# Compressed keys behind every block of the window keys: one logit product for two attention branches

## The chip, the cores and the metric

The program runs on one core of one Trainium2 chip. The core's engines run beside each other, each with its own queue of instructions: PE (TensorE) multiplies matrices, ACT (ScalarE) applies functions, DVE (VectorE) and POOL (GpSimd) work element by element, and SP (SyncE) issues transfers between the chip's memory and the on-chip memory. The metric is the time of one execution in microseconds; less is better.

## The reference

One transformer block on a sequence of 1024 tokens with a model width of 1024: a norm, one large input projection, two mixers beside each other (an mLSTM and a sparse attention), a gated merge of both, and a feed-forward network. The change lies in the sparse attention. It has 8 query heads of width 64 in 2 key groups, and for each query it sums three branches:

```python
def block(i):
    ...
    lc = (jnp.einsum('bgrqd,bgcd->bgrqc', qb, kc_).astype(jnp.float32)
          + table[:, :, rel_bucket(t[:, None] - cmp_end[None, :])])
    p_c = masked_softmax(lc, cmp_end[None, :] <= t[:, None])
    o_c = jnp.einsum('bgrqc,bgcd->bgrqd', p_c, vc_.astype(jnp.float32))
    ...
    ls = jnp.einsum('bgrqd,bgqnd->bgrqn', qb, k_g).astype(jnp.float32) + bias_s
    p_s = masked_softmax(ls, mask_s[:, :, None])
    o_s = jnp.einsum('bgrqn,bgqnd->bgrqd', p_s, v_g.astype(jnp.float32))
    ...
    lw = jnp.einsum('bgrqd,bgkd->bgrqk', qb, k_wb).astype(jnp.float32) + table[:, :, rel_bucket(dist)]
    p_w = masked_softmax(lw, mask_w)
    o_w = jnp.einsum('bgrqk,bgkd->bgrqd', p_w, v_wb.astype(jnp.float32))
    gb = lax.dynamic_slice_in_dim(gates, qs, Q, axis=3)
    return gb[..., 0:1] * o_c + gb[..., 1:2] * o_s + gb[..., 2:3] * o_w
```

The compressed branch (c) attends to 63 compressed keys, each made from 32 tokens by a small network. The selected branch (s) attends to the top 16 blocks of 64 tokens; with 1024 tokens these are all blocks, so it is plain causal attention. The window branch (w) attends to the last 512 tokens. `masked_softmax` divides by `max(sum, 1e-30)`, and `gates` is a sigmoid of a projection.

## The kernel before

**Stages.** The program runs in stages, one after the other with some overlap: the norm and the transposed input; the projections and the mLSTM; B2, which makes the queries of the attention and the compressed keys and values; C, the attention; the rest of the merge, the output projection and the feed-forward network. Each product in high precision is made from parts: a float32 operand is split into a rounded high part and the low rest (names in `H`/`hi` and `L`/`lo`), and a product is two or three matmuls.

**B2** (from some 315 to 380 us). `b2_dense` makes the four query tiles `nq`, each in two halves of 512 tokens. A half comes out of PSUM by ACT as `st` (printed as `snq`), DVE rounds it to `hnq` and takes the rest `lnq`, and SP stores both to memory (`d_qh`, `d_ql`). Beside it, `compress` adds positions to the raw keys (`fl`, sixteen DVE steps), multiplies with `w_cmp1` (`ph`) and writes the compressed keys as `KHC` and `KLC` (64 columns for each key group) and the values as `VHC`. Weights stream in through `raw` tiles, loaded by SP in pieces of 512 bytes, and are split into `whi` (ACT) and `wlo` (DVE or, in C, POOL). After the first query tile, `load_pair(0)` asks POOL's queue for the queries of the first pair of heads (`QA`) and the keys of the first group (`KH`, `KL`, in rows of 4 KB; j = 1 are the window's, j = 0 the selected branch's), and SP's for the tables of position biases (`FB`, `FW`).

**C** (from some 382 to 707 us) has 32 units: 4 pairs of heads p, and for each the 8 blocks i of 128 queries in the order 0, 7, 1, 6, 2, 5, 3, 4. A unit u has five jobs: the window product for both heads, the compressed product for both heads together, the selected product for both heads. A job runs on PE (`s_job`: L974 and L975 with the high and low keys, L960 and L961 with the compressed ones, into a PSUM tile `S`), on DVE (L987: add the bias, clip, row minimum into `nx`) and on ACT (L991: exponential and row sum `sm`). `scale` makes the factor `rs` = gate / max(sum, 1e-30) in three DVE steps (L1003 to L1005), once for the window and compressed branch and once for the selected one, and multiplies it in. `t_job` transposes the weights on PE (`T`, L1043), copies them as `TH` (ACT, L1048) and `TL` (DVE, L1052), and multiplies with the values into `obank` (L1063, L1065); ACT takes the result out as `os` (L1071), and SP stores it.

**The order in C** is set when the program is built, by a list scheduler: each operation has an engine, an assumed duration and what it depends on, and the operation that can start first is emitted next. Where PE would wait, `place_dense` puts in three matmuls of the merge projection (`d`, nine tiles, 420 matmuls in C) as filler; a tile's half leaves as `mg` (L922). When the last product of a pair has been read by DVE, `load_pair` asks for the next pair's data, and for new keys after the second pair.

## Time and profile before

| | |
|---|---|
| median of 3 runs | 1622.4 us (1619.43 to 1623.4) |
| profiled execution, its own time | 1624.57 us |
| span of its trace | 1622.8 us |
| granted PE clock, mean | 0.991 |
| busy share of the span | PE 97%, DVE 66%, ACT 46%, POOL 13% |
| chain that ended last | PE 82%, DVE 4%, DMA 3%, ACT 1% |

The span is the time from the first to the last instruction of one profiled execution on the slowest core. A busy time adds up the durations of an engine's instructions, and PE's matmuls overlap, so the distance from one start to the next says more about their price than their duration. A wait is the idle time of an engine before an instruction, put down to what ended it.

### The profile page before, as it was taken

What the parts mean: (1) busy time and instruction counts of PE and PEld (TensorE: products, weight loads), DVE (VectorE), ACT (ScalarE), POOL (GpSimd) and SP (SyncE); (2) the same over time, 40 slices, a digit from 0 to 9 for tenths busy, and PEclk for the clock granted to TensorE, in tenths of its full rate; (3) what the DMA queues carried; (4) which work ended last, traced back from release to release, by engine and by line L of the source; (5) the groups of instructions that cost most, each with busy time, mean ns of one, the idle gap of its engine ahead of it and who ended that gap; (6) DMA issues with size and microseconds to landing.
All of it is one profiled execution on the core that took longest, in us unless ns stands there. A gap on an engine that the chain in (4) does not pass through costs nothing.

```text
span 1622.8 us, 22113 instructions
## 1 busy us (share of the span) xinstructions
PE 1572.2 (97%) x7938; PEld 1327.5 (82%) x7938; DVE 1066.4 (66%) x2276; ACT 746.6 (46%) x1561; POOL 204.5 (13%) x225
## 2 busy tenths in 40 slices
PE   6999999989999999999999998999999999999997
PEld 6876888878989888988887887888888888888876
DVE  6456553245888687952355378666676666978996
ACT  5225455325878687853334344333333333454443
POOL 4002333310102110012000014000000000000130
PEclk9999999999999999999999999999999999999999
DMA  8003532782233422154447222222332223741202
GB/s 251 7 22 97 150 116 96 240 242 70 67 101 82 125 66 82 40 173 148 143 139 255 74 85 85 78 87 89 118 103 78 79 78 104 285 166 42 98 7 104
DMA packets 143773, 181.43 MB, mean 112 GB/s; under 512 B 10414, under 2 KB 100944, under 8 KB 143664
## 3 DMA queue, kind: packets, MB, share of 16 engines
q1 hardware_dynamic: 137440, 157.31, 31.5%
q0 software_dynamic: 5888, 22.06, 4.8%
q8 instruction: 62, 1.02, 0.3%
q10 hardware_dynamic: 336, 0.66, 0.1%
q14 instruction: 47, 0.39, 0.1%
HBM read 137.95 MB, written 49.90 MB: 116 GB/s over the span
## 4 chain that ended last, share of the span: by engine, by line
PE 82%; DVE 4%; DMA 3%; ACT 1%; issue 1%; SPq 0%; POOL 0%; DVEq 0%; ACTq 0%
PE PS L271 14%; PE PS L272 14%; PE PS L270 14%; PE d L270 6%; PE d L272 6%; PE d L271 6%; PE T L1043 4%; PE obank L1063 2%; PE obank L1065 2%; PE br L270 1%; PE br L271 1%; PE br L272 1%; DMA raw<-in_w_in 1%; PE pn L696 1%; DMA q<-d_yn 0%
## 5 line engine op out<-in xcount | busy, mean ns | idle before, releaser
L270 PE MATMUL d<-UTH,whi 128*128 128x512 f32 x576 | 235.1, 408 | 3.4 <-ACT snq L846 2.4
L272 PE MATMUL d<-UTH,wlo 128*128 128x512 f32 x576 | 227.1, 394 | 1.1 <-POOL wlo L249 1.1
L271 PE MATMUL d<-UTL,whi 128*128 128x512 f32 x576 | 226.1, 393 | 0.0
L1421 DVE TENSOR_TENSOR sl<-PS,sl 128x512 f32<-128x512 f32 x182 | 124.0, 688 | 100.2 <-PE PS L272 98.4
L272 PEld LDWEIGHTS d<-UTH,wlo 128*128 128x128 f32 x576 | 108.9, 189 | 26.1 <-POOL wlo L249 1.9
L270 PEld LDWEIGHTS d<-UTH,whi 128*128 128x128 f32 x576 | 109.2, 190 | 21.9 <-ACT snq L846 3.0
L249 POOL TENSOR_TENSOR wlo<-raw,whi 128x1024 fp32r<-128x1024 f32 x31 | 76.2, 2458 | 402.5 <-ACT whi L247 308.2
L271 PEld LDWEIGHTS d<-UTL,whi 128*128 128x128 f32 x576 | 109.6, 190 | 17.6
L1052 DVE TENSOR_TENSOR TL<-T,TH 128x512 fp32r<-128x512 f32 (+1 forms) x184 | 103.7, 583 | 20.9 <-ACT TH L1048 19.5
L1048 ACT ACTIVATE TH<-T 128x512 fp32r<-128x512 f32 (+1 forms) x184 | 90.8, 511 | 34.4 <-PE T L1043 31.6
L1421 DVE TENSOR_TENSOR sl<-sl,sl 128x512 f32<-128x512 f32 (+1 forms) x113 | 77.3, 691 | 18.3 <-ACT sl L1424 12.9
L1424 ACT ACTIVATE sl<-sl 128x512 f32<-128x512 f32 (+1 forms) x85 | 53.5, 631 | 69.8 <-PE PS L271 47.6
L1063 PE MATMUL obank<-TH,VHL 128*128 128x256 f32 x264 | 76.4, 312 | 0.0
L1424 ACT ACTIVATE wh<-sl 128x512 fp32r<-128x512 f32 x61 | 38.5, 631 | 81.9 <-PE PS L271 71.6
L1421 POOL TENSOR_TENSOR acc<-acc 128x512 f32<-128x512 f32 x6 | 9.2, 1548 | 503.5 <-DVE acc L1421 503.4
L1065 PE MATMUL obank<-TL,VHL 128*128 128x256 f32 x264 | 68.5, 282 | 0.0
L270 PE MATMUL PS<-q 128*128 128x512 f32 x172 | 66.9, 389 | 0.0
L271 PE MATMUL PS<-q 128*128 128x512 f32 x172 | 66.9, 389 | 0.0
L272 PE MATMUL PS<-q 128*128 128x512 f32 x172 | 66.9, 389 | 0.0
L1383 DVE TENSOR_TENSOR q<-br,q 128x512 f32<-128x512 f32 x32 | 21.9, 688 | 67.3 <-ACT q L1376 47.0
L1424 ACT ACTIVATE q<-sl 128x512 fp32r<-128x512 f32 x74 | 43.4, 624 | 46.5 <-PE PS L271 29.1
L1421 DVE TENSOR_TENSOR q<-sl,q 128x512 fp32r<-128x512 f32 x72 | 50.3, 736 | 2.9 <-ACT q L1424 2.9
(1418 smaller groups left out, 4302.0 us busy)
## 6 DMA issues: line engine op xcount, KB each, us to landing
raw<-in_w_in SPq DMA_DIRECT2D x40, 512.0 KB, 4.7
ra<-in_w_gate SPq DMA_DIRECT2D x22, 512.0 KB, 5.3
d_gu<-sl SPq DMA_DIRECT2D x44, 256.0 KB, 2.1
q<-d_mg SPq DMA_DIRECT2D x32, 256.0 KB, 3.2
d_rep<-d_row POOLq DMA_DIRECT2D x8, 960.0 KB, 10.0
sl<-d_gu SPq DMA_DIRECT2D x15, 512.0 KB, 5.3
sl<-in_w_down SPq DMA_DIRECT2D x15, 512.0 KB, 5.2
ra<-in_w_up SPq DMA_DIRECT2D x11, 512.0 KB, 3.8
```

Of the source, the lines that this page charges most:

```text
L249: eng.tensor_tensor(lo, v, cast32(hi), ALU.subtract)
L270: nc.tensor.matmul(ps, ah, bh, start=first, stop=False)
L271: nc.tensor.matmul(ps, ah, bl, start=False, stop=False)
L272: nc.tensor.matmul(ps, al, bh, start=False, stop=last)
L1043: nc.tensor.transpose(pt[:, z, P * r:P * r + P], e, ident)
L1048: nc.scalar.activation(hl[0][:, 0:m], pt[:, 0:m], AF.Copy)
L1052: nc.vector.tensor_tensor(hl[1][:, 0:m], pt[:, 0:m], cast32(hl[0])[:, 0:m], ALU.subtract)
L1063: nc.tensor.matmul(po, vv, th[:, z, :], start=(st[1] == 0), stop=False)
L1065: nc.tensor.matmul(po, vv, tl[:, z, :], start=False, stop=(st[1] == st[2]))
L1383: nc.vector.tensor_tensor(sg[b], ps, sg[b], ALU.mult)
L1421: return pl.step(alts, lambda e: ENG[e].tensor_tensor(out_(), x(), y(), alu), reads, writes, **kw)
L1424: return pl.step((("ACT", cost),), lambda e: nc.scalar.activation(out_(), x(), fn), reads, writes, **kw)
```

## The change

The tile of the window keys gets 192 instead of 128 columns for each block of 128 keys. The new function `behind` copies the group's 64 compressed keys behind each of the eight blocks on POOL: for the first group after B2, for the second in `load_pair`. The last block of a window product then is 192 columns wide and gives the logits of the window and of the compressed branch for that head at once; the compressed product as a job of its own goes. The earlier blocks of the window stand in a product of their own. The loads of the window keys, split in blocks now, move in pieces of 512 bytes. The gates are inverted once after the sigmoid, so that a factor is 1 / (max(sum, 1e-30) x inverted gate): one fused DVE step and a reciprocal in place of three. Five tiles lose a buffer: `lnq` and `snq` in B2, `mg` and `os` in C. The scheduler's assumed durations are changed with it, and with them its order.

```diff
@@ -30,6 +30,7 @@
...
 FX = 1152
+KB = 192
...
@@ -633,6 +634,7 @@
...
             nc.scalar.activation(GT[:, :, 0:24], GT[:, :, 0:24], AF.Sigmoid)
+            nc.vector.reciprocal(GT[:, :, 0:24], GT[:, :, 0:24])
...
@@ -802,6 +804,11 @@
...
+    def behind(g):
+
+        for t_, c_ in zip(KS[g, 1], (KHC, KLC)):
+            nc.gpsimd.tensor_copy(t_[:, :, P:KB], c_[:, g, None, :].to_broadcast([P, NT, KB - P]))
+
     def load_pair(p):
         g = p // 2
         for r in range(2):
@@ -812,14 +819,16 @@
             QA[h] = q
         if p % 2 == 0:
             for j in (1, 0):
-                kh = kq.tile([P, T], F32R, name=f"KH{g}{j}", tag=f"KH{j}", bufs=1)
-                kl = kq.tile([P, T], F32R, name=f"KL{g}{j}", tag=f"KL{j}", bufs=1)
+                m = KB if j == 1 else P
+                kh = kq.tile([P, NT, m], F32R, name=f"KH{g}{j}", tag=f"KH{j}", bufs=1)
+                kl = kq.tile([P, NT, m], F32R, name=f"KL{g}{j}", tag=f"KL{j}", bufs=1)
                 gs = slice(64 * g, 64 * g + 64)
-                nc.gpsimd.dma_start(kh[0:64, :], d_kh[j][gs, :])
-                nc.gpsimd.dma_start(kh[64:128, :], d_kh[j][gs, :])
-                nc.gpsimd.dma_start(kl[0:64, :], d_kl[j][gs, :])
-                nc.gpsimd.dma_start(kl[64:128, :], d_kl[j][gs, :])
+                for t_, d_ in ((kh, d_kh), (kl, d_kl)):
+                    for z in range(2):
+                        nc.gpsimd.dma_start(t_[64 * z:64 * z + 64, :, 0:P], d_[j][gs, :].rearrange("p (b c) -> p b c", c=P))
                 KS[g, j] = (kh, kl)
+            if g > 0:
+                behind(g)
...
@@ -841,8 +850,8 @@
                 def evict(ps, half):
                     hs = slice(512 * half, 512 * half + 512)
                     hi = bp.tile([P, 512], F32R, name=f"h{nm}{j}{half}", tag="sh", bufs=2)
-                    lo = bp.tile([P, 512], F32R, name=f"l{nm}{j}{half}", tag="sl", bufs=2)
-                    st = bp.tile([P, 512], F32, name=f"s{nm}{j}{half}", tag="st", bufs=2)
+                    lo = bp.tile([P, 512], F32R, name=f"l{nm}{j}{half}", tag="sl", bufs=1)
+                    st = bp.tile([P, 512], F32, name=f"s{nm}{j}{half}", tag="st", bufs=1)
...
@@ -905,6 +914,7 @@
...
         driver(b2_dense(), compress())
+        behind(0)
...
@@ -915,7 +925,7 @@
...
-    def merge_tile(j, sp, psp, bufs, tag="mg", tbufs=2):
+    def merge_tile(j, sp, psp, bufs, tag="mg", tbufs=1):
...
@@ -950,37 +960,38 @@
...
             s = psC.tile([P, T], F32, name=f"S{u}{kind}{r}", tag="S", bufs=2)
-            if kind == "c":
-                n8, nn = 8 * i + 8, ncmp(i)
-                e = cp.tile([P, 2, P], F32, name=f"E{u}c", tag="Ec", bufs=3)
-                nc.gpsimd.memset(e[:, :, nn:P], 0.0)
-                EX[u, "c"] = e
-                for q in range(2):
-                    o = s[:, 64 * q:64 * q + n8]
-                    nc.tensor.matmul(o, QA[2 * p + q][:, cs], KHC[:, g, 0:n8], start=True, stop=False)
-                    nc.tensor.matmul(o, QA[2 * p + q][:, cs], KLC[:, g, 0:n8], start=False, stop=True)
+            b = 1 if kind == "s" else 2
+            kh, kl = KS[g, b - 1]
+            q_ = QA[2 * p + r]
+            e = cp.tile([P, T if b == 1 else 640], F32, name=f"E{u}{kind}{r}", tag="E" + kind, bufs=4)
+            EX[u, kind, r] = e
+            f = FB[2 * p + r]
+
+            def logits(o, k_, last):
+                nc.tensor.matmul(o, q_[:, cs], k_(kh), start=True, stop=False)
+                nc.tensor.matmul(o, q_[:, cs], k_(kl), start=False, stop=True)
+
+            if b == 1:
+                n, o0 = P * (i + 1), 0
+                for c0 in range(0, i + 1, 4):
+                    m = min(4, i + 1 - c0)
+                    logits(s[:, P * c0:P * (c0 + m)], lambda k: k[:, c0:c0 + m, :], False)
+                rows_ = []
+            else:
+
+                nw = nwin(i)
+                n, o0 = P * nw, P if nw == 4 else 0
+                if nw > 1:
+                    logits(s[:, o0:o0 + n - P], lambda k: k[:, i + 1 - nw:i, 0:P], False)
+                logits(s[:, o0 + n - P:o0 + n - P + KB], lambda k: k[:, i, :], True)
+                if r == 0:
+                    EX[u, "c"] = cp.tile([P, 2, P], F32, name=f"E{u}c", tag="Ec", bufs=3)
+                ec, nn = EX[u, "c"], ncmp(i)
+                nc.gpsimd.memset(ec[:, r, nn:P], 0.0)
                 y0 = 31 + 16 * (56 - 8 * i)
-                rows_ = [(e[:, q, 0:nn], s[:, 64 * q:64 * q + nn], FB[2 * p + q][:, y0:y0 + 16 * (nn - 1) + 1:16], q, 0)
-                         for q in range(2)]
-                cost = 4 * 107.0
-            else:
-                b = 1 if kind == "s" else 2
-                n, k0 = (P * (i + 1), 0) if b == 1 else (P * nwin(i), P * max(0, i - 4))
-                kh, kl = KS[g, b - 1]
-                q_ = QA[2 * p + r]
-                cost = 0.0
-                for c0 in range(0, n, 512):
-                    m = min(512, n - c0)
-                    nc.tensor.matmul(s[:, c0:c0 + m], q_[:, cs], kh[:, k0 + c0:k0 + c0 + m], start=True, stop=False)
-                    nc.tensor.matmul(s[:, c0:c0 + m], q_[:, cs], kl[:, k0 + c0:k0 + c0 + m], start=False, stop=True)
-                    cost += 2 * max(107.0, m / 2.4)
-                e = cp.tile([P, T if b == 1 else 640], F32, name=f"E{u}{kind}{r}", tag="E" + kind, bufs=4)
-                EX[u, kind, r] = e
-                if b == 1 or i < 4:
-                    bias = FB[2 * p + r][:, 896 - P * i:896 - P * i + n]
-                else:
-                    bias = FW[2 * p + r]
-                rows_ = [(e[:, 0:n], s[:, 0:n], bias, r, b)]
+                rows_ = [(ec[:, r, 0:nn], s[:, o0 + n:o0 + n + nn], f[:, y0:y0 + 16 * (nn - 1) + 1:16], r, 0)]
+            bias = f[:, 896 - P * i:896 - P * i + n] if b == 1 or i < 4 else FW[2 * p + r]
+            rows_.insert(0, (e[:, 0:n], s[:, o0:o0 + n], bias, r, b))
...
-            return cost, low, exp
+            return low, exp
...
@@ -1000,9 +1011,8 @@
...
             def first():
                 rs, sm = RS[u][:, :, sl], SUM[u][:, :, sl]
-                nc.vector.tensor_scalar(rs, sm, 1.0e-30, None, ALU.max)
+                nc.vector.scalar_tensor_tensor(rs, sm, 1.0e-30, gt, ALU.max, ALU.mult)
                 nc.vector.reciprocal(rs, rs)
-                nc.vector.tensor_tensor(rs, rs, gt, ALU.mult)
...
@@ -1064,7 +1074,7 @@
...
                 if last:
-                    os_ = cp.tile([P, 256], F32, name=f"os{u}", tag="os", bufs=3)
+                    os_ = cp.tile([P, 256], F32, name=f"os{u}", tag="os", bufs=2)
...
@@ -1106,15 +1116,19 @@
...
-            for k, r in (("w", 0), ("w", 1), ("c", 0), ("s", 0), ("s", 1)):
-                b = {"w": 2, "c": 0, "s": 1}[k]
+            for k, r in (("w", 0), ("w", 1), ("s", 0), ("s", 1)):
+                b = {"w": 2, "s": 1}[k]
...
                 def emit(u=u, k=k, r=r, box=box):
-                    _, box["low"], box["exp"] = s_job(u, k, r)
-
-                n = 126 if k == "c" else (P * (i + 1) if b == 1 else P * nwin(i))
-                cost = 428.0 if k == "c" else 2 * sum(max(107.0, min(512, n - c) / 2.4) for c in range(0, n, 512))
+                    box["low"], box["exp"] = s_job(u, k, r)
+
+
+                if b == 1:
+                    n, parts = P * (i + 1), [min(512, P * (i + 1) - c) for c in range(0, P * (i + 1), 512)]
+                else:
+                    n, parts = P * nwin(i), [P * (nwin(i) - 1)] * (nwin(i) > 1) + [KB]
+                cost = 2 * sum(max(109.0, m / 2.4 + 13.0) for m in parts)
...
@@ -1125,16 +1139,16 @@
...
                 so = push(Op("PE", cost, deps, emit, (u, 1)))
                 chain["S"] = [so]
-                nr = 2 if k == "c" else 1
-                tt = push(Op("DVE", nr * (80.0 + 1.044 * (n / nr)), [so], lambda box=box: box["low"](), (u, 1)))
+                nr, n = (2, n + ncmp(i)) if b == 2 else (1, n)
+                tt = push(Op("DVE", nr * 180.0 + 1.044 * n, [so], lambda box=box: box["low"](), (u, 1)))
                 s_free.append(tt)
-                ex = push(Op("ACT", nr * (290.0 + 0.833 * (n / nr)), [tt], lambda box=box: box["exp"](), (u, 1)))
+                ex = push(Op("ACT", nr * 290.0 + 0.833 * n, [tt], lambda box=box: box["exp"](), (u, 1)))
                 ops[k, r] = ex
-                if k == "c" or (k == "s" and r == 1):
-                    part = 0 if k == "c" else 1
-                    de = [ops["w", 0], ops["w", 1], ex] if part == 0 else [ops["s", 0], ex]
+                if r == 1:
+                    part = 0 if k == "w" else 1
+                    de = [ops[k, 0], ex]
                     todo = scale(u, part)
-                    rs = push(Op("DVE", 600.0, de, todo[0][0], (u, 2)))
+                    rs = push(Op("DVE", 400.0, de, todo[0][0], (u, 2)))
                     bl = [2, 2, 0, 0] if part == 0 else [1, 1]
                     scd = {}
...
@@ -1241,7 +1255,7 @@
...
-        todo_pair = {p: sum(1 for u in range(NU) if units[u][0] == p) * 5 for p in range(4)}
+        todo_pair = {p: sum(1 for u in range(NU) if units[u][0] == p) * 4 for p in range(4)}
```

What it does to the order is seen in three places. The first is PE in C at the second window product of unit 3 (block 6, head 1; `S3w` is its PSUM tile), before and after:

```order
L974 MATMUL S3w_3510<-KH_2880,QA_2877 128x512
L975 MATMUL S3w_3510<-KL_2881,QA_2877 128x512
L974 MATMUL S3w_3510<-KH_2880,QA_2877 128x128
L975 MATMUL S3w_3510<-KL_2881,QA_2877 128x128
L960 MATMUL S3c_3519<-KHC,QA_2874 128x56
L961 MATMUL S3c_3519<-KLC,QA_2874 128x56
L960 MATMUL S3c_3519<-KHC,QA_2877 128x56
L961 MATMUL S3c_3519<-KLC,QA_2877 128x56
```

```order
L971 MATMUL S3w_3509<-KH_2881,QA_2878 128x512
L972 MATMUL S3w_3509<-KL_2882,QA_2878 128x512
L971 MATMUL S3w_3509<-KH_2881,QA_2878 128x192
L972 MATMUL S3w_3509<-KL_2882,QA_2878 128x192
L271 MATMUL d_1_3353<-UTH,whi_3129 128x512
L272 MATMUL d_1_3353<-UTL,whi_3129 128x512
L273 MATMUL d_1_3353<-UTH,wlo_3130 128x512
```

The 128 columns of the last block became 192, and the four matmuls with `KHC` and `KLC` are gone; filler (`d`) and transposes follow directly.

The second is DVE in B2, from the third `lnq` to the fifth, with the semaphores that each waits for (those named DMAHW are landings of SP's transfers), before and after:

```order
L848 TENSOR_TENSOR lnq_2954<-snq_2955,hnq_2953 128x512 [waits DMAHW6_49,DVE_49]
L847 CAST hnq_2998<-snq_3000 128x512 [waits DMAHW7_49,Activation_49]
L848 TENSOR_TENSOR lnq_2999<-snq_3000,hnq_2998 128x512 [waits DMAHW0_49,DVE_49]
L249 TENSOR_TENSOR wlo_3027<-raw_2904,whi_3026 128x1024 [waits DMAHW5_49,PE_49,Activation_49]
L898 TENSOR_TENSOR KLC<-po_3033,KHC 128x2x63 [waits Activation_49]
L847 CAST hnq_3043<-snq_3045 128x512 [waits DMAHW6_49,Activation_49]
L848 TENSOR_TENSOR lnq_3044<-snq_3045,hnq_3043 128x512 [waits DMAHW7_49,DVE_49]
```

```order
L857 TENSOR_TENSOR lnq_2955<-snq_2956,hnq_2954 128x512 [waits DMAHW0_49,DVE_49]
L856 CAST hnq_2999<-snq_3001 128x512 [waits DMAHW7_49,Activation_49]
L857 TENSOR_TENSOR lnq_3000<-snq_3001,hnq_2999 128x512 [waits DMAHW7_49,DVE_49]
L250 TENSOR_TENSOR wlo_3028<-raw_2905,whi_3027 128x1024 [waits DMAHW5_49,PE_49,Activation_49]
L907 TENSOR_TENSOR KLC<-po_3034,KHC 128x2x63 [waits Activation_49]
L856 CAST hnq_3044<-snq_3046 128x512 [waits DMAHW6_49,Activation_49]
L857 TENSOR_TENSOR lnq_3045<-snq_3046,hnq_3044 128x512 [waits DMAHW1_49,DVE_49]
```

Each `lnq` waits for the landing that its successor waited for before: that of the transfer of the half just before it. The first `fl` no longer waits for a transfer itself, since the `lnq` ahead of it does.

The third is PE at the end of C, from the last matmul of filler on, before and after:

```order
L272 MATMUL d_1_7434<-UTH,wlo_6712 128x512
L1043 MATMUL T_2_7715<-cst,E31w_7522 128x128
L1043 MATMUL T_2_7715<-cst,E31w_7565 128x128
L1063 MATMUL obank<-TH_0_7701,VHL 128x256
L1065 MATMUL obank<-TL_0_7711,VHL 128x256
L1063 MATMUL obank<-TH_0_7701,VHL 128x256
L1065 MATMUL obank<-TL_0_7711,VHL 128x256
L1043 MATMUL T_3_7728<-cst,E31c 128x128 x2
L1063 MATMUL obank<-TH_1_7713,VHL 128x256
L1065 MATMUL obank<-TL_1_7724,VHL 128x256
```

```order
L273 MATMUL d_1_7225<-UTH,wlo_6658 128x512
L1053 MATMUL T_2_7501<-cst,E30c 128x128 x2
L1073 MATMUL obank<-TH_0_7486,VHL 128x256
L1075 MATMUL obank<-TL_0_7497,VHL 128x256
L1073 MATMUL obank<-TH_0_7486,VHL 128x256
L1075 MATMUL obank<-TL_0_7497,VHL 128x256
L1053 MATMUL T_3_7511<-cst,E30s_7292 128x128
L1053 MATMUL T_3_7511<-cst,E30s_7332 128x128
L1053 MATMUL T_3_7511<-cst,E30s_7292 128x128
L1053 MATMUL T_3_7511<-cst,E30s_7332 128x128
```

Before, 35 rows follow the last filler, all of the last unit, 31; now 70 follow, from the compressed weights of unit 30 on.

## Rows read from the trace of the kernel before

**Rows 1.** The page: span and busy time of each engine.
```profile
span 1622.8 us, 22113 instructions
...
PE 1572.2 (97%) x7938; PEld 1327.5 (82%) x7938; DVE 1066.4 (66%) x2276; ACT 746.6 (46%) x1561; POOL 204.5 (13%) x225
```

**Rows 2.** Busy times by stretch; PEclk, DMA share and GB/s at the end.
```profile
330.00:356.00 26.00, 25.39 (x129) 21.24 (x127) 8.37 (x23) 4.82 (x7) 7.49 (x12) 1.00 1.08 278
380.00:707.00 327.00, 320.06 (x2128) 286.98 (x2128) 271.68 (x907) 258.53 (x678) 39.02 (x61) 1.00 0.30 76
699.95:707.16 7.21, 5.07 (x38) 4.26 (x37) 3.79 (x7) 3.85 (x9) 0.00 (x0) 1.00 0.19 55
```

**Rows 3.** PE in order of time, 399.9 to 403.3: start us, length us.
```profile
399.91 0.28 PE L974 MATMUL S2s<-KH,QA 128*128 128x256 f32 x1
...
400.14 0.40 PE L974 MATMUL S3w<-KH,QA 128*128 128x512 f32 x1
...
400.60 0.22 PE L974 MATMUL S3w<-KH,QA 128*128 128x128 f32 x1
...
400.77 1.11 PE L1043 MATMUL T<-cst,E1s 128*128 128x128 f32 x8
...
402.82 0.24 PE L960 MATMUL S3c<-KHC,QA 128*128 128x56 f32 x1
...
403.24 0.66 PE L1043 MATMUL T<-cst,E1s 128*128 128x128 f32 x4
```

**Rows 4.** DVE by line in the attention stage: busy us, mean ns.
```profile
L1005 DVE TENSOR_TENSOR rs<-rs,GT 128x4 f32<-128x4 f32 x64 | 12.8, 199 | 2.2
```

**Rows 5.** DVE and POOL in order of time, 555 to 561 us.
```profile
556.41 2.16 DVE L1003 TENSOR_SCALAR rs<-sm 128x4 f32<-128x4 f32 x1
...
555.74 2.41 POOL L249 TENSOR_TENSOR wlo<-raw,whi 128x1024 fp32r<-128x1024 f32 x1 [19.55 <-ACT whi L247]
```

**Rows 6.** POOL in order of time; the idle time before, with its releaser, in brackets.
```profile
381.27 2.38 POOL L249 TENSOR_TENSOR wlo<-raw,whi 128x1024 fp32r<-128x1024 f32 x1 [34.28 <-DVE lnq L848]
...
533.43 2.38 POOL L249 TENSOR_TENSOR wlo<-raw,whi 128x1024 fp32r<-128x1024 f32 x1 [5.65 <-ACT whi L247]
```

**Rows 7.** Three transfers by line, 330 to 350 us, then all of d_ql: issue, median to landing.
```profile
L851 SPq DMA_DIRECT2D d_ql<-lnq x1: 319/319/319, 338.0 to 338.0; - x1
...
DMA to landing us min/median/max: 18.7/18.7/18.7
...
L231 SPq DMA_DIRECT2D raw<-in_w_in x1: 433/433/433, 334.3 to 334.3; - x1
...
DMA to landing us min/median/max: 21.2/21.2/21.2
...
L818 POOL DMA_DIRECT2D KH<-d_kh x2: 517/607/697, 336.7 to 342.5; - x2
...
DMA to landing us min/median/max: 9.7/10.2/10.7
...
d_ql<-lnq SPq DMA_DIRECT2D x8, 256.0 KB, 3.2
```

**Rows 8.** SP's queue in order of time.
```profile
359.46 1.20 SPq L877 DMA_DIRECT2D w<-in_w_cmp  x2
```

**Rows 9.** DVE in order of time, 345 to 359 us.
```profile
345.48 0.69 DVE L848 TENSOR_TENSOR lnq<-snq,hnq 128x512 fp32r<-128x512 f32 x1
...
357.71 0.28 DVE L898 TENSOR_TENSOR KLC<-po,KHC 128x126 fp32r<-128x126 f32 x1
...
358.37 0.69 DVE L848 TENSOR_TENSOR lnq<-snq,hnq 128x512 fp32r<-128x512 f32 x1
```

**Rows 10.** Waits of PE, 356 to 370 and 385 to 710: us, times, longest.
```profile
PE ph L887 <- DMA w<-in_w_cmp: 3.8, 1, 3.8
PE d L270 <- ACT snq L846: 1.9, 1, 1.9
...
PE T L1043 <- DVE E17w L1013: 1.2, 1, 1.2
```

## The prediction

> **What bounds the kernel now.** I read the page first [rows 1]: TensorE (PE) is busy 1572.2 of 1622.8 us. So a time saved counts if it is PE's own work, or if it ends a wait of PE. Then I asked for busy times by stretch [rows 2]. In the attention stage, 380 to 707 us, PE is busy 320.06 of 327.00 us at full clock, DVE 271.68 and ACT 258.53: PE is the bound, with 6.94 us of idle in 327. In the stage before it (B2, here 330 to 356) PE is busy too, 25.39 of 26, but the DMA share is 1.08 at 278 GB/s: transfers queue there. PE's rows in order of time [rows 3] give what a logit product costs, and the rows on transfers and waits around 334 to 364 us [rows 7 to 10] show two waits of PE, which the change touches by its smaller buffers.
>
> **The products of the logits.** A busy time counts overlapping matmuls twice, so I price them by the distance between starts. In [rows 3] four matmuls of the compressed branch (56 columns) run from 402.82 to 403.24: 0.42, or 0.105 each, though they have few columns. A hi/lo pair of 512 columns takes 400.14 to 400.60 = 0.46, one of 256 399.91 to 400.14 = 0.23, one of 128 400.60 to 400.77 = 0.17.
> Removed: 2 heads x 2 (hi, lo) x 32 units = 128 matmuls of the compressed branch, 128 x 0.105 = -13.4 us. Widths run from 8 to 64 columns; four of the narrowest could cost less than those of 56, so I allow -11.5 to -13.7.
> Added: 64 more columns in each window product, and another cut of the window. A pair of 192 columns must lie between the 0.17 of 128 and the 0.23 of 256; I take 0.20, halfway. A pair of 384 lies halfway between 256 and 512, 0.35. There are 8 window jobs for each query block i (4 head pairs x 2 heads):
> i >= 4 (32 jobs): 512+128 becomes 512+192, +0.03 (0 to 0.06), +1.0 us.
> i = 3: 512 becomes 384+192, 0.55 - 0.46 = +0.09. i = 2: 384 becomes 256+192, 0.43 - 0.35 = +0.08. i = 1: 256 becomes 128+192, +0.14. i = 0: 128 becomes 192, +0.03. Together 8 x 0.34 = +2.7.
> Sum of PE work: -13.4 + 3.7 = -9.7 us, with bounds -7 and -11.5. Transposes, value products and the 420 matmuls of merge filler are the same in number.
>
> **Vector work.** The three short steps of a weight factor become two: 64 x 199 ns = 12.8 us off DVE [rows 4], or nothing if the fused step takes as long as the two it replaces. DVE isn't the bound, so I put this at 0. Its cover is PE's own work: where DVE is late, PE waits. The one such place that I can explain is at 559.62: POOL splits a weight for 2.41 us from 555.74, a step of 4 elements (L1003) takes 2.16 on DVE meanwhile [rows 5], where one of the like takes 0.2 [rows 4], and PE waits 1.2 us for what follows [rows 10]. Such meetings come by chance of the order; the new order may move each on or off the path. I take 0, from -2 to +3. The one new reciprocal in the gates stands in front of DVE's wait for the summed chunk states, and has 192 elements, against 0.69 us for a step of 512 [rows 9]: 0, or 0.7 at most without that wait.
>
> **The copies behind the keys.** Each reads 64 columns eight times, 512 elements; POOL's 1024-element step takes 2.38 [rows 6], so I put one at 1.2 (0 to 2.4), four in all. The first two can run when the compressed keys are ready (low halves at 357.71, [rows 9]); POOL has nothing to do until its step at 381.27, with which the attention stage begins. Cover 20 us, cost 0. Behind them on POOL stand a weight split and memsets. The other two follow the loads of the second key group; there POOL sits idle 5.65 us until 533.43 for a weight's high half [rows 6], so the two fit and push nothing. Cost 0; without the cover it would be 2.4 each time.
>
> **The end of the stage.** The list scheduler has the same filler but places it earlier: after the last dense matmul stood 35 rows, now 70. There PE depends on the ring transpose, ACT, DVE, value product. In that stretch of before, 699.95 to 707.16 [rows 2], PE is busy 5.07 of 7.21 us and loses 2.1. With twice the rows a loss at the same rate would be 2.1 more; but part of it stands at the stage's last step, which comes once, so I take half, +1.0 (0 to +2.2).
>
> **B2: single buffers.** Room for the longer keys is made by cutting the tile of the low halves (`lnq`) and of the raw query sums (`snq`) from two buffers to one. Each `lnq` now waits until the transfer just before it has landed, not the one before that. For most halves that is nothing, but `d_ql` issued at 338.0 took 18.7 us [rows 7], so it landed at 356.7. The next `lnq`, which ran at 345.48 [rows 9], now starts at 356.7. Behind it on DVE: the split of a weight, `KLC`, `hnq`, `lnq` of the next half, then `fl`. On SP its two transfers hold back a weight load and, further on, both loads of `w_cmp1` issued at 359.46 [rows 8], which PE already awaits for 3.8 us [rows 10]. Count on: `lnq` ends at 357.4, split 358.6, `KLC` 358.9, `hnq` 359.3. The next `lnq` needs the transfer issued at about 357.8; at the median such a transfer lands in 3.2 [rows 7], so it starts near 361.0 instead of 358.37 [rows 9]. Everything behind it is 2.6 later, so is `w_cmp1`, and so is PE: +2.6 (to +4.5 if the weight load, now issued beside it, takes its share).
> Against this: the loads of the window keys now come in pieces of 512 bytes instead of 4 KB. In [rows 7] the weight load of 512-byte pieces issued at 334.3 took 21.2 us, while two key loads issued after it, at 336.7 and 342.5, landed within 10.7. The large pieces pushed past the small ones. With equal pieces the weight load and the `d_ql` behind it land some us earlier, and the wait shrinks or goes. I take +1.3, halfway between none and 2.6; bounds -3.4 and +4.5. The rest (one `mg`, two `os` buffers) frees its tile when a store of at most 256 KB has landed; if that takes the 3.2 of `d_ql`, it lies within the 24 matmuls of the next half, 24 x 0.23 = 5.5 us by [rows 3], or within a unit of attention, 327 / 32 = 10 us: 0.
> The Trainium skill ("DMA: Bandwidth & Descriptors", section "Why small descriptors are slow (HBM only)") has a fixed cost per packet, some 3 cycles on 16 for 512 bytes; by that rule the 1 MB of window keys would take about a sixth longer, an estimate from the page, and the wait would grow by under 1 us. In its section "Queues, rings and completion order" the queues take turns packet by packet; by that rule the weight load gains, as in the rival "early landing". The trace has the second effect, at 21.2 against 10.7 us, and no row shows the first.
>
> **Sum.** -9.7 + 0 + 0 + 1.0 + 1.3 = -7.4 us. The profiled execution took 1624.6 us (1622.8 of span and 1.8 around it), which gives 1617.2; the runs' median, 1622.4, lies 2.2 lower, so I forecast 1615.0.
>
> **The rivals.**
> Buffer wait: `w_cmp1` is late by the full 4.5, and PE too. For it: every step stands in the queue rows. Against: the earlier landings. -9.7 + 1.0 + 4.5 = -4.2: 1618.
> Attention no longer limited by PE: the filler is gone early, T tiles have two buffers, and meetings of POOL and DVE move onto the path: +3 there and +2.2 at the end. For it: DVE is busy 83% of the stage already. Against: it loses work too. -9.7 + 5.2 + 1.3 = -3.2: 1619.
> Early landing: the weight load comes in 5 us or more earlier; PE's wait of 1.9 for `snq` [rows 10] goes, and 1.5 of that for `w_cmp1`. -9.7 + 1.0 - 3.4 = -12.1: 1610.
> Slower: the transfer that the later `lnq` waits for is slow again. If the one issued at 357.8 takes 18.7 us like that of 338.03, `lnq` starts at 376.5 instead of 358.37, and `w_cmp1` with it: +18. -9.7 + 1.0 + 18 = +9.3: 1632. It decides from a delay of 14 us on (slower by 0.3%). Against: by then the keys' loads are nearly through, and the median landing is 3.2 [rows 7].
> The change does nothing: if the short matmuls lay hidden under weight loads that remain, removing them would save nothing. Against: PE's starts move on by 0.105 for each, and their weight loads go with them. 1624, 2 in 100.
>
> **How the numbers follow.** The forecast has 0.49, buffer wait 0.17, attention 0.13, early landing 0.13, slower 0.06, nothing 0.02. The bound for a real difference is 0.3%, 4.9 us: faster is below 1617.5. The forecast's own range is 1612 to 1618; I count 0.45 of its 0.49 as faster, all of early landing, 0.05 of the buffer wait and 0.03 of the attention rival: 0.66. Slower 0.06; the same 0.28. The range reaches to the early landing below (1610) and past the attention rival above (1621); outside stay the rest of these, the slower case and that of no effect, 2 in 10.
>
> **What would show it.** Right: in the attention stage PE's busy time falls, no row of S and c, window products of 192 columns 0.09 to 0.11 apart, stage shorter by 7 to 10 us; PE's wait for `w_cmp1` near 5 us, `lnq` starting with the landing of `d_ql`. DVE some 12 us less busy in the stage, without effect on the end. Wrong: a 192-column pair at 0.3 or more (the added work doubles), many new waits of T for `TL` after the last filler, or a wait for `w_cmp1` of 10 us.

## The result and the profile after

The change made the kernel faster: 1606.6 us (median of 5 runs, 1605.0 to 1608.0) against 1622.5 (5 runs, 1619.4 to 1623.4). The ratio is 0.9904, with a 95% interval of 0.9891 to 0.9918: 15.9 us, where 7.4 were forecast. The measured time lies outside the stated range.

The page of the changed kernel, span and busy times, beside [rows 1]; the profiled execution took 1606.7 us:

```profile
span 1604.9 us, 21900 instructions
...
PE 1558.6 (97%) x7858; PEld 1316.0 (82%) x7858; DVE 1053.1 (66%) x2214; ACT 742.1 (46%) x1560; POOL 209.7 (13%) x261
```

Where the time went is seen by laying one point of the program in both traces beside the other. The first window product came at 382.93 and now at 381.83 (-1.1); the first filler after the last value product at 707.16 and now 691.74 (-15.4 in all); the end lies 17.9 us earlier. So the attention stage gave 14.3 of the 17.9 us between the two spans, B2 and what is ahead of it 1.1, and everything behind the attention 2.5. Busy times by stretch of the changed kernel, in the columns of [rows 2]:

```profile
330.00:356.00 26.00, 26.00 (x133) 22.05 (x132) 10.26 (x26) 5.90 (x9) 9.09 (x14) 1.00 1.24 278
380.00:690.00 310.00, 306.96 (x2037) 275.19 (x2036) 255.25 (x842) 252.18 (x674) 42.52 (x93) 1.00 0.34 80
679.40:691.74 12.34, 9.73 (x74) 8.44 (x73) 8.50 (x20) 8.62 (x20) 0.00 (x0) 1.00 0.11 33
```

In the attention stage PE now idles 3.0 of 310 us, where it was 6.9 of 327. Counted between the two points above, and with waits over 0.15 us alone, it is 3.3 where it was 6.9; 2.6 of the 3.3 stand in the last 12.3 us, after the filler has run out. PE's waits between the two points:

```profile
PE T L1053 <- DVE TL L1062: 1.7, 4, 0.6
PE d L271 <- ACT mg L932: 0.7, 2, 0.4
PE d L271 <- ACT os L1081: 0.5, 1, 0.5
PE obank L1075 <- DVE TL L1062: 0.5, 1, 0.5
```

Four waits of the kernel before, 3.8 us together, are gone. They stood there near 559, 598 and 635 us, for the scaling by a factor, for `TL` and for `nx`:

```profile
559.62 1.45 PE L1043 MATMUL T<-cst,E17w 128*128 128x128 f32 x8 [1.17 <-DVE E17w L1013]
...
598.38 0.44 PE L1043 MATMUL T<-cst,E20s 128*128 128x128 f32 x2 [1.54 <-DVE TL L1052]
...
634.48 0.53 PE L1043 MATMUL T<-cst,E24w 128*128 128x128 f32 x2 [0.41 <-DVE E24w L1013]
...
636.68 0.49 PE L974 MATMUL S25s<-KH,QA 128*128 128x512 f32 x1 [0.67 <-DVE nx L987]
```

PE in the changed kernel, in order of time at the same unit as in [rows 3]:

```profile
398.70 0.40 PE L971 MATMUL S3w<-KH,QA 128*128 128x512 f32 x1
...
399.16 0.25 PE L971 MATMUL S3w<-KH,QA 128*128 128x192 f32 x1
399.25 0.28 PE L972 MATMUL S3w<-KL,QA 128*128 128x192 f32 x1
399.36 1.08 PE L1053 MATMUL T<-cst,E1s 128*128 128x128 f32 x8
```

The pair of 512 columns takes 0.46 as before, the pair of 192 0.20, as estimated. Summed over the stage by the distance between starts, with waits taken out, the window products cost 35.2 us (31.2 before), the selected ones 36.3 (36.7), and the compressed ones, 13.3, are gone: -9.7, as forecast. The other three kinds (filler, transposes, value products) took 235.1 us instead of 236.2, with the same 420 filler matmuls.

B2, DVE in order of time, to be laid beside [rows 9]; under it the weight load of [rows 7] with its landing, and PE's longest wait there:

```profile
349.73 0.69 DVE L857 TENSOR_TENSOR lnq<-snq,hnq 128x512 fp32r<-128x512 f32 x1 [4.56 <-DMA d_ql<-lnq]
...
357.49 0.69 DVE L857 TENSOR_TENSOR lnq<-snq,hnq 128x512 fp32r<-128x512 f32 x1 [5.41 <-DMA d_ql<-lnq]
```

```profile
L232 SPq DMA_DIRECT2D raw<-in_w_in x1: 653/653/653, 333.7 to 333.7; - x1
...
DMA to landing us min/median/max: 14.2/14.2/14.2
```

```profile
PE ph L896 <- DMA w<-in_w_cmp: 5.9, 1, 5.9
```

Both things that the prediction set against each other are there: the single buffer is waited for, twice, 10.0 us of DVE in all; and the weight load lands after 14.2 instead of 21.2 us. PE waits 5.9 us for `w_cmp1`, where it was 3.8, and 0.5 for the query sums, where it was 2.4.

Behind the attention both kernels do the same matmuls. Laid beside each other one by one, 2.0 of the 2.5 us come at one place, where PE waits for `q`: 2.2 us before, 1.8 after. In the first of these two profiles the granted clock (last but two in the row) falls to half behind that wait, in the second it does not:

```profile
866.00:886.00 20.00, 17.80 (x71) 14.23 (x71) 12.44 (x14) 9.05 (x12) 0.00 (x0) 0.91 0.83 278
```

```profile
848.00:868.00 20.00, 18.18 (x81) 14.73 (x80) 13.72 (x16) 10.22 (x15) 0.00 (x0) 1.00 0.83 273
```

Other runs of the old work have no such fall there, and some of the new work have one. So these 2.5 us are scatter between executions.

### The profile page after: what moved, and what is told of

The parts are those of the page before. It is cut to its first block, busy times and chain, and to the rows that moved or that the text cites. A ratio compares the mean times of both kernels' runs of the same rounds, so it can differ in the third digit from the quotient of the medians.

```text
span 1604.9 us, 21900 instructions
## 1 busy us (share of the span) xinstructions
PE 1558.6 (97%) x7858; PEld 1316.0 (82%) x7858; DVE 1053.1 (66%) x2214; ACT 742.1 (46%) x1560; POOL 209.7 (13%) x261
## 3 DMA queue, kind: packets, MB, share of 16 engines
q8 instruction: 62, 1.02, 0.3%
## 4 chain that ended last, share of the span: by engine, by line
PE 83%; DVE 3%; DMA 2%; ACT 1%; issue 1%; POOL 0%; SPq 0%; DVEq 0%; ACTq 0%
PE PS L272 15%; PE PS L271 15%; PE PS L273 15%; PE d L271 7%; PE d L273 6%; PE d L272 6%; PE T L1053 4%; PE obank L1075 2%; PE obank L1073 2%; PE br L272 1%; PE br L271 1%; PE br L273 1%; DMA d_ql<-lnq 1%; PE pn L698 1%; DMA raw<-in_w_out 0%
## 5 line engine op out<-in xcount | busy, mean ns | idle before, releaser
L1435 DVE TENSOR_TENSOR sl<-sl,sl 128x512 f32<-128x512 f32 (+1 forms) x113 | 77.3, 690 | 17.9 <-ACT sl L1438 12.2
```

Of the source, the lines that this page charges most:

```text
L1435: return pl.step(alts, lambda e: ENG[e].tensor_tensor(out_(), x(), y(), alu), reads, writes, **kw)
```

## The experiments

Two questions stood open after the result: whether the idle time left the attention stage with the work or with the order that the scheduler happened to draw; and why B2 lost nothing, though its buffer wait is there. Theories A, B and C are named anew in each expectation. Ratios are to the kernel before on the same chip, with a 95% interval. Two lengths are read from PE's rows: **B2** is the distance from the first product of the compression (`ph`) to the first window product; **stage C** goes from there to the first filler after the last value product. Idle counts PE's waits over 0.15 us.

**Single buffers alone.** The kernel before with

```diff
-tag="sl", bufs=2
+tag="sl", bufs=1
-tag="st", bufs=2
+tag="st", bufs=1
```

> The kernel before with one buffer instead of two for the low halves and the raw query sums, and nothing else of the change. Theory A (each low half waits for the landing of the transfer just before it): the step that ran at 345.5 us starts at about 356.7, when the slow transfer (18.7 us) lands; PE's wait for the second weights of the compression grows from 3.8 to 6 us or more, and the first window product, before at 382.9, comes 2 to 4.5 us later; the run is about 2.5 us slower than before. Rival B (the buffer is never waited for, since the weight load that holds everything lands at 355.5 anyway): first window product within 0.5 us of 382.9, time unchanged.

Measured: 1624.0 us, ratio 1.0010 (0.9999 to 1.0021). The low half waits 10.8 us for the landing, as expected, and starts at 356.4; PE's wait for the weights grows from 3.8 to 4.2 us only, and B2 from 49.3 to 49.9. The next low half lost little: the transfer that it needs landed in time for 359.5, not 361.0. `w_cmp1` is asked for 1.1 us later than before. The wait is real; in B2 it costs some 0.5 us, not 2.6, and by the whole runs it can't be told from none.

**Pieces of 512 bytes alone.** The kernel before with

```diff
-kh = kq.tile([P, T], F32R, ...)
...
-nc.gpsimd.dma_start(kh[0:64, :], d_kh[j][gs, :])
...
+m = 136 if j == 1 else P
+kh = kq.tile([P, NT, m], F32R, ...)
...
+nc.gpsimd.dma_start(t_[64 * z:64 * z + 64, :, 0:P], d_[j][gs, :].rearrange("p (b c) -> p b c", c=P))
```

> The kernel before with the window keys in a tile whose blocks are 136 columns apart (8 of them unused), so that their loads move in pieces of 512 bytes; all else as before. Theory A (large pieces push past the small ones in a shared queue): the weight load issued near 334 us lands after some 14 us instead of 21, the wait of 1.9 us for the query sums goes, and the first window product comes 1 to 4 us earlier than 382.9; time 1 to 4 us less. Rival B (the landing came earlier for another reason): it lands after 20 us or more again, and nothing moves.

Measured: 1621.3 us, ratio 0.9997 (0.9987 to 1.0006). The weight load lands after 17.0 us instead of 21.2 and the wait for the query sums goes, as theory A has it. Yet B2 is 49.3 us, as before: both `w_cmp1` loads, issued at 353.5, 6 us earlier, now take 9.3 us to land instead of 4.6, and PE goes on at 362.97. So `w_cmp1` lands at 362.9 us, before at 364.1, though it was asked for 6 us earlier. That PE waits for the end of a queue of transfers, whichever stands last in it, fits this; the run with early weights, below, tests it.

**Both.** The kernel before with the two edits together:

```diff
-tag="sl", bufs=2
+tag="sl", bufs=1
-tag="st", bufs=2
+tag="st", bufs=1
-kh = kq.tile([P, T], F32R, ...)
+m = 136 if j == 1 else P
+kh = kq.tile([P, NT, m], F32R, ...)
...
```

> The kernel before with both: single buffers and window keys in pieces of 512 bytes (blocks 136 columns apart). Theory: what the change did to the stage before the attention is these two and nothing else, so the first window product comes within 0.5 us of 381.8, where the changed kernel has it, and PE waits about 5.9 us for the second weights of the compression. Rival: the copies behind the keys or the gates have a part; then it differs by more than 0.5 us.

Measured: 1621.7 us, ratio 0.9995 (0.9985 to 1.0004); the weight load lands after 14.4 us, PE waits 5.7 us for the weights, and the first window product comes at 380.8, B2 47.9 us. That is 1.0 us off the 381.8 expected, twice the bound: 0.4 stand ahead of B2 and 0.6 in it, though the stage agrees with the changed kernel (48.6) in every wait to 0.2 us. How far B2 scatters for the same code is seen in two runs below that don't touch it (x4 and x11: 49.2 and 47.9), so none of these differences can be told from none.

**Inverted gates alone.** The kernel before with

```diff
+nc.vector.reciprocal(GT[:, :, 0:24], GT[:, :, 0:24])
-nc.vector.tensor_scalar(rs, sm, 1.0e-30, None, ALU.max)
+nc.vector.scalar_tensor_tensor(rs, sm, 1.0e-30, gt, ALU.max, ALU.mult)
 nc.vector.reciprocal(rs, rs)
-nc.vector.tensor_tensor(rs, rs, gt, ALU.mult)
```

> The kernel before with the inverted gates alone: one reciprocal more, 64 of the three-step factors become two steps; the scheduler's numbers and so the order are untouched. Theory A (DVE is not the bound; PE's idle in the attention stage comes from three factor steps held by a weight split on POOL): DVE loses 12 to 13 us, the collisions near 556 and 632 us stay, the one near 595, in the step that goes, may go: the time falls by 0 to 1.5 us. Rival B (the two-step factor is what took the idle away): PE idle in the attention stage falls from 6.9 to about 3.4 and the time by 3 us or more.

Measured: 1618.3 us, ratio 0.9972 (0.9962 to 0.9983). Stage C falls by 2.0 us, from 324.2 to 322.2: 1.4 of idle (6.85 to 5.45) and 0.6 of PE's pace. The run gains 4.5 us, more than the 0 to 1.5 expected, and 2.0 of it are seen in the stage. The long steps near 556 and 632 stay, at 1.77 and 1.02 us. The long factor step near 595 is gone, but the split now holds the step behind it, and PE waits there 1.54 us as before:

```profile
593.15 3.08 DVE L1013 TENSOR_SCALAR E21w<-E21w,rs 128x640 f32<-128x640 f32 x1
```

```profile
593.11 2.39 POOL L249 TENSOR_TENSOR wlo<-raw,whi 128x1024 fp32r<-128x1024 f32 x1 [22.46 <-DVE rs L1005]
```

The 1.4 us of idle went in part at the two other meetings: the wait of 1.17 is 0.60, that of 0.41 is gone, that of 0.67 is 0.47. So the step that I put at 0 is worth 2 us in the trace; rival B's 3.4 of idle did not come.

**The change without inverted gates.** The changed kernel with

```diff
-nc.vector.reciprocal(GT[:, :, 0:24], GT[:, :, 0:24])
-nc.vector.scalar_tensor_tensor(rs, sm, 1.0e-30, gt, ALU.max, ALU.mult)
+nc.vector.tensor_scalar(rs, sm, 1.0e-30, None, ALU.max)
 nc.vector.reciprocal(rs, rs)
+nc.vector.tensor_tensor(rs, rs, gt, ALU.mult)
```

> The changed kernel with the three-step factors of before (gates not inverted), with the new scheduler's numbers and so the order of the change. Theory A (the inversion saves only DVE time that hides): DVE 12 us busier, time within 1.5 us of the changed kernel, unless the third step meets a split. Rival B (the shorter chain to the transposes is worth time): 3 us or more slower than the changed kernel.

Measured: 1609.4 us, ratio 0.9931 (0.9916 to 0.9947) against 0.9904 of the change. Stage C is 312.4 instead of 309.9 us, 0.8 of the 2.5 idle. By the ratios the run is 4.4 us slower than the change, so theory A, which allowed 1.5, falls. Both ways round the inversion is worth 2 to 2.5 us in the stage.

**Splits of the attention stage on DVE.** The kernel before with

```diff
-yield from fm_tile(j_mg[j], psp, "D", bufs, evict, pool=True, mark=True)
+yield from fm_tile(j_mg[j], psp, "D", bufs, evict, pool=j >= NMC, mark=True)
```

> The kernel before with the weight splits of the attention stage on DVE instead of POOL; the order is otherwise the same. It does the whole computation. Theory A (a factor step on DVE that starts during a POOL split is held until the split ends, and 3.8 of the 6.9 us of PE idle come from three such meetings): no factor step over 0.4 us is left, the three waits of PE near 559, 598 and 635 us (3.8 us together) go; nine splits of 1.2 us now stand on DVE, so new waits of up to 2 us may come: time 0 to 4 us less. Rival B (the long steps come from something else on DVE): two or three factor steps over 1 us stay and PE idle stays near 6.9.

Measured: 1629.8 us, ratio 1.0057 (1.0042 to 1.0072). Without a split on POOL no factor step of the stage is longer than 0.23 us, and the waits for a factor's scaling are gone; but the nine splits on DVE bring new waits, up to 2.2 us, and idle in stage C is 13.3 us. The cause of the long steps is confirmed. The gain of 0 to 4 us that I expected is not there: the cure costs more.

**Splits twice.** The changed kernel with

```diff
 eng.tensor_tensor(lo, v, cast32(hi), ALU.subtract)
+if pool:
+    eng.tensor_tensor(lo, v, cast32(hi), ALU.subtract)
```

> The changed kernel with each weight split on POOL in the attention stage done twice in a row (the second writes the same values again). Theory A (meetings by chance): POOL's splits now cover 4.8 instead of 2.4 us each; a factor step that starts in one is held to its end, in a fused step with two operands from the on-chip memory as in the single ones; one to four steps over 0.4 us appear, and PE idle in the attention stage rises from 3.3 by 1 to 5 us. Rival B (the fused step cannot be held, so that the change cured the collisions): no factor step over 0.4 us, PE idle within 0.5 of 3.3.

The splits on POOL ahead of the attention were doubled with it, which cost 23 us up to the first product of the compression (356.3 instead of 333.3) and most of the run's 28 (1635.1 us, ratio 1.0088, 1.0073 to 1.0103); so only stage C is read. There four fused steps are held for 0.48 to 1.58 us, and one for 0.34, where the changed kernel had none over 0.17, and idle rises from 3.3 to 4.4. One of them on DVE, and POOL's second split under it:

```profile
606.80 1.58 DVE L1016 SCALAR_TENSOR_TENSOR rs<-sm,GT 128x4 f32<-128x4 f32 x1
```

```profile
605.96 2.40 POOL L252 TENSOR_TENSOR wlo<-raw,whi 128x1024 fp32r<-128x1024 f32 x1
```

605.96 + 2.40 = 608.36, and the step ends at 608.38: it was held to the split's end. The fused step is as open to it as the single ones, so the change did not cure the meetings; its order has none between a split and a factor step. The changed kernel does have one between DVE and its own copies behind the second group's keys: three scaling steps from 520.68 us on are held by them, some 1.0 us in all, and PE does not wait there:

```profile
520.68 0.82 DVE L1023 TENSOR_SCALAR E15w<-E15w,rs 128x640 f32<-128x640 f32 x1
521.43 1.14 DVE L1023 TENSOR_SCALAR E15c<-E15c,rs 128x39 f32<-128x39 f32 x2
```

```profile
521.15 0.81 POOL L810 CAST KH<-KHC 128x512 fp32r<-128x512 f32 x1
521.92 0.60 POOL L810 CAST KL<-KLC 128x512 fp32r<-128x512 f32 x1
```

**The same work in other orders.** Three runs keep the changed kernel's work and give the scheduler old numbers: all three (x8), the one of a product (x14), the one of a factor (x15); a fourth (x12) takes the old one of a bias step.

```diff
-cost = 2 * sum(max(109.0, m / 2.4 + 13.0) for m in parts)
+cost = 2 * sum(max(107.0, m / 2.4) for m in parts)
-tt = push(Op("DVE", nr * 180.0 + 1.044 * n, ...
+tt = push(Op("DVE", nr * 80.0 + 1.044 * n, ...
-rs = push(Op("DVE", 400.0, ...
+rs = push(Op("DVE", 600.0, ...
```

> The changed kernel, ordered with the old numbers for a product, a bias step (80 instead of 180 ns each) and a factor (600 instead of 400 ns); the work is the same. Theory A (the new numbers matter only through which meetings and waits fall on the path): PE's work in the attention stage is the same within 1 us, PE idle anywhere from 3 to 8 us, so the time is 0 to 5 us more than the changed kernel's. Rival B (the new numbers are what makes PE's work cheaper, by fewer changes from one kind of product to the other): the pace of the filler rises by 0.002 us or more for each matmul, 1 us in all.

> The changed kernel with the old number for a bias step alone (80 ns instead of 180 ns beside its length). Theory A (the 8 us that the old numbers cost come from a scheduler that thinks DVE faster than it is): idle in the attention stage 5 us or more above the 3.3 of the change. Theory C (chance of the order): filler lasts to the end here (2 rows behind it), so the waits at the end go, and idle is 2 to 6 us.

> The changed kernel, ordered with the old number for a product alone; the work is the same. Theory C (each set of numbers gives another order, and how many waits an order meets is a draw): idle in the attention stage between 3 and 9 us, with other places of waiting; 151 rows stand behind the last filler, so 3 to 5 us at the end. Theory A (the work itself took the idle away): idle within 1 us of the 3.3 of the change.

> The changed kernel, ordered with the old number for a factor alone (600 instead of 400 ns); the work is the same. Theory C (draw): idle in the attention stage between 3 and 9 us; 35 rows stand behind the last filler, so some 2 us at the end, the rest by meetings with POOL's splits. Theory A: idle within 1 us of 3.3.

Measured (us; idle and the rest are PE's, in stage C):

| kernel | time | ratio (95%) | idle | the rest |
|---|---|---|---|---|
| before | 1622.5 | 1 | 6.9 | 317.4 |
| changed kernel | 1606.6 | 0.9904 (0.9891 to 0.9918) | 3.3 | 306.6 |
| x8, all three | 1612.8 | 0.9952 (0.9935 to 0.9969) | 8.9 | 309.1 |
| x12, bias step | 1608.2 | 0.9918 (0.9903 to 0.9933) | 5.7 | 306.9 |
| x14, product | 1615.2 | 0.9956 (0.9940 to 0.9971) | 8.6 | 310.3 |
| x15, factor | 1612.5 | 0.9937 (0.9920 to 0.9954) | 9.1 | 308.3 |

(x12 has 12 filler matmuls less in the stage; 12 x 0.233 = 2.8 us are added to its rest.) The waits of x8 and of x14 are others than before: in x8 one of 3.4 us, for `mg`, at 541 us; in x14 ten for `TL`, the longest 0.95. The first two rows of x8's waits, and ACT at the long one:

```profile
PE d L271 <- ACT mg L932: 4.0, 3, 3.4
PE T L1053 <- DVE TL L1062: 3.9, 6, 1.1
```

```profile
540.63 0.69 ACT L932 ACTIVATE mg<-d,COLS 128x512 f32<-128x512 f32 x1 [4.82 <-DMA d_mg<-mg]
```

That is the single `mg` buffer: its store, issued at 524.5, lands after 16.1 us, and ACT and then PE wait for it. In x14 two fused steps meet a split and are held 2.38 us each, and two scaling steps 2.37; in x15 three steps that scale weights are held, one of them 2.94 us where the like takes 0.55:

```profile
480.42 2.38 DVE L1014 SCALAR_TENSOR_TENSOR rs<-sm,GT 128x2 f32<-128x2 f32 x1
```

```profile
552.66 0.18 DVE L1015 RECIPROCAL rs<-rs 128x4 f32<-128x4 f32 x1
552.88 2.94 DVE L1023 TENSOR_SCALAR E17w<-E17w,rs 128x640 f32<-128x640 f32 x1
```

So idle in the stage is 3.3, 5.7, 8.6, 8.9 and 9.1 us for the same work in five orders, and the change's own is the best of them. Three things make the difference that can be counted: the idle behind the last filler (2.6 in the changed kernel, none in x12, 4.7, 3.4 and 3.0 in x8, x14 and x15), the steps held by splits (none in the changed kernel, two in x12, none, four and three in x8, x14 and x15), and the wait for `mg`. The rest moves too, by 3.7 us; why stays open. Of the expectations, those of theory C held for x12 and x14; x15 lies 0.1 us above its range of idle and x8 0.9 above, and the rest of x8 moved by 2.5 us, where 1 was expected.

**The old work with new numbers.** The kernel before with

```diff
-cost = 428.0 if k == "c" else 2 * sum(max(107.0, min(512, n - c) / 2.4) ...
+cost = 436.0 if k == "c" else 2 * sum(max(109.0, min(512, n - c) / 2.4 + 13.0) ...
-tt = push(Op("DVE", nr * (80.0 + 1.044 * (n / nr)), ...
+tt = push(Op("DVE", nr * 180.0 + 1.044 * n, ...
```

> The kernel before, its work unchanged, ordered with the new numbers for a product and a bias step (the factor's number stays, since it still has three steps). Theory A (the new numbers alone make a better order): PE idle in the attention stage falls below 5 us, time 2 us or more less than before. Theory C (numbers and work belong together, the order's waits are by chance): idle between 5 and 12 us, here rather more, since 186 rows stand behind the last filler; time from 1 us less to 5 us more.

Measured: 1626.9 us, ratio 1.0037 (1.0024 to 1.0050); idle 9.4 us, the rest 320.9. The time is 6 us more, just past the 5 expected. The new numbers are not a better description that would pay by itself: with the old work they draw a worse order. Theory A falls.

**Early weights.** The changed kernel with the loads of the compression's weights placed earlier on SP's queue, into the same three buffers.

```diff
...
+load_w1(0, 0)
+load_w1(0, 1)
+load_w1(1, 0)
 yield 12000.0
...
 nc.tensor.matmul(ph[:, 0:126], w1[o // 8][:, o % 8, :], ...
+if j == 0 and o == 7:
+    load_w1(1, 1)
```

> The changed kernel with the four weight loads of the compression placed earlier in SP's queue: three before the compression begins, the fourth after the first two thirds of its first half, so that all are under way before the queue around 335 to 357 us fills. Theory A (in that stretch the transfers are limited by their sum, so whatever stands last is late, whichever buffer it waits for): PE's wait of 5.9 us for these weights falls below 1 us, and since PE doesn't stand still there its clock stays up; the first window product comes 4 to 7 us earlier than the 48.6 us after the first product of the compression; the run is 3 to 7 us faster than the changed kernel. Rival B (something else is as late, the positions added on DVE or the query halves): the wait moves there and under 2 us are won.

Two more build on it, each on the one ahead: a tenth merge tile as filler, and the position steps of the second compression ahead of the next low half (the first compression no longer yields behind `KLC`).

```diff
-NMC = 9
+NMC = 10
```

> As the run with the early weights, and ten instead of nine merge tiles may be used as filler in the attention stage, so that filler lasts to its end (2 rows behind the last filler instead of 70). Theory A (the 2.6 us of idle in the last 12 us come from the lack of filler): idle in the stage falls from 3.3 to some 1 us, 1 to 2.5 us faster than without. Rival B (the tenth tile's weights and its buffers bring new waits): nothing or a loss.

```diff
 nc.vector.tensor_tensor(KLC[:, :, 0:NCMP], p3, cast32(KHC)[:, :, 0:NCMP], ALU.subtract)
+continue
```

> As the run with the early weights and the tenth tile, and the sixteen position steps of the second compression stand on DVE directly behind the compressed keys, ahead of the next low half of the queries. Theory A (with the weights there, PE now waits 3 to 4 us for these steps, which stand behind a low half that waits for its single buffer): that wait of PE goes, the first window product comes 2 to 4.5 us earlier against the first product of the compression than the 45.7 us of the run before it, and the run is 2 to 4 us faster. Rival B (the query halves are then as late): the wait moves to the sums of the queries, and under 1 us is won.

Measured: 1603.3 us, ratio 0.9885 (0.9866 to 0.9904) with the early weights; 1600.5, 0.9872 (0.9856 to 0.9888) with `NMC = 10` as well; 1595.4, 0.9830 (0.9815 to 0.9845) when the position steps also come ahead of the low half. B2 is 48.6 us in the changed kernel, 43.3, 45.7 and 40.0 in these, so the last step won 5.7 us there, more than the 2 to 4.5 expected; idle in stage C is 3.3, 3.3, 0.9 and 0.9. With early weights PE waits for the position steps instead; of its waits between 334 and 380 us the longest, in the three kernels in turn:

```profile
PE ph L902 <- DVE fl L898: 3.0, 1, 3.0
```

```profile
PE ph L902 <- DVE fl L898: 4.1, 1, 4.1
```

```profile
PE d L271 <- ACT snq L855: 0.5, 1, 0.5
```

The third has no wait for `ph` left. The stretch from 356 to 370 us in the changed kernel, and in that third one:

```profile
356.00:370.00 14.00, 8.11 (x33) 6.73 (x32) 6.62 (x20) 1.68 (x2) 0.55 (x2) 0.76 0.72 207
```

```profile
356.00:370.00 14.00, 13.54 (x75) 11.29 (x74) 4.21 (x7) 3.58 (x7) 0.07 (x1) 1.00 0.61 194
```

PE does 75 matmuls in the 14 us, in place of 33. On the mean of the stretch the granted clock is 1.00, where it was 0.76 with the wait of 5.9 us in it. The single buffer's wait, hidden behind the late weights in the change, is what was left once they were early, and moving the steps ahead of it takes it off the path. This version beats both kernels, by 27 us the one before.

## Why the prediction was right in its parts and wrong in its size

**Products: right.** -9.7 forecast, -9.7 measured; the pair of 192 columns at 0.20.

**Vector work and the end of the stage: the step that failed.** "I take 0, from -2 to +3" for the meetings and +1.0 for the end; PE's idle in the stage fell by 3.5. The end did cost 0.5 more: 2.6 idle in the last 12.3 us against 2.1 in 7.2. But the four waits near 559, 598 and 635 us went, 3.8 us in all. I had named the mechanism for the first, 1.2 us; in the trace of before the others follow a factor step held by a split in the same way, 2.37 and 1.40 us long:

```profile
594.92 2.37 DVE L1005 TENSOR_TENSOR rs<-rs,GT 128x4 f32<-128x4 f32 x1
...
632.29 1.40 DVE L1003 TENSOR_SCALAR rs<-sm 128x4 f32<-128x4 f32 x1
```

```profile
594.87 2.39 POOL L249 TENSOR_TENSOR wlo<-raw,whi 128x1024 fp32r<-128x1024 f32 x1 [22.46 <-ACT whi L247]
...
630.89 2.39 POOL L249 TENSOR_TENSOR wlo<-raw,whi 128x1024 fp32r<-128x1024 f32 x1 [24.68 <-PE S24s L975]
...
633.38 0.28 POOL L956 MEMSET E26c<- 128x226 f32 x1
```

So the lower bound of -2 was too near: two thirds of what the meetings cost stood in the trace and I had not read them. The Trainium skill ("SBUF — State Buffer", section "Who interferes with whom") has such a lock between DVE and GpSimd, held for the whole instruction; the trace agrees, to 0.02 us in the run with two splits.

What is more, I priced one order. The five orders of the same work give 0.9904 to 0.9956, that is 7 to 16 us of gain; three of the five gain 7 to 10, and the forecast of 7.4 lies among these. That it does is luck in part: in stage C these three gain 5.3 to 6.9 us, where the forecast had 8.7 (-9.7 and +1.0); their idle rose by some 2 us and the inverted gates gave 2 to 2.5, which I had at 0. Idle is 7.1 us on the mean of the five orders, close to the 6.9 of before. So a large part of the size missed is the draw of this order: 3.3 of idle, and a rest of 306.6 where the others have 306.9 to 310.3. Whether the change's numbers would draw well again for other work is open; for the old work they did not.

**Inverted gates: mis-sized.** 0 forecast, 2 to 2.5 us in stage C. The reason, that DVE isn't the bound, does not hold: PE waits for DVE at single places, and with one step less some of these waits were shorter. In part this is the meetings again. The `tensor_scalar` step of before was held 0.4 us past the split, to the end of the memset behind it (633.66, and the step ends at 633.69); the fused step in the run with inverted gates alone went when the split ended (556.99 and 557.01). By whole runs the gates are worth 4.5 and 4.4 us; where the other two lie is not settled.

**B2: both mechanisms right, the sum wrong.** +1.3 forecast; the changed kernel shows -0.8, and by the runs with equal code it can't be told from 0. Each low half waits for its landing, and the pieces of 512 bytes let the weight load land 7 us earlier. Of the rival "early landing" the first half came: PE's wait for `snq` went from 2.4 to 0.5 us; but that for `w_cmp1` grew by 2.1. The step that failed is "so is `w_cmp1`, and so is PE": the loads of `w_cmp1` land at 362 to 365 us in five kernels (before, changed, and those with single buffers, with small pieces and with both), whether they are issued at 353.5 or at 360.6. With single buffers alone they are 1.1 us later asked for and 1.3 later there, half of the 2.6.

**Copies, reciprocal, fewer `mg` and `os` buffers: right at 0 for this order.** The copies took 0.61 and 0.75 us at 349 to 353 and no engine waited for them; the second pair held DVE for some 1.0 us and PE did not wait. `mg` is waited for 0.7 us in stage C, 0.5 before. But I reckoned a store of `mg` at 3.2 us; in x8 one took 16.1, and the single buffer cost PE 3.4 us. That it costs nothing is so in the order that was drawn, not in each.

**Sum.** Products -9.7, other matmuls -1.1, idle -3.5, B2 -0.75 and -0.35 ahead of it: -15.4 at the end of the stage. Behind it the span lost 2.5 us more, for the most part by the clock of one profile; the medians differ by 15.9.

## What to carry to other kernels

Where a scheduler written into the kernel sets the order, the order is a draw of its own: a change of work should be measured in several orders, and a forecast should carry the scatter between them (here 3 to 9 us of idle in five) and not the idle of the one order that is seen. Read what ends each wait of the bound engine, all of them and not the largest, before a bound is put on what a new order may win. And when a wait for a transfer lies in a stretch where transfers queue, a buffer or a piece size may hardly move it (here by 1 us or so); placing the load ahead of the stretch won 5 us of B2 and 3 us of the run.
